# Modulation columns by one-column matmuls, later stores of three weight blocks, and weight subtractions on GpSimd

## The chip, the core and the metric

The kernel runs on one core of one Trainium2 chip. The metric is the device time of one execution in microseconds (us). A core has five engines that run side by side: TensorE (PE in the profile; its weight loads are a row of their own, PEld), VectorE (DVE), ScalarE (ACT), GpSimd (POOL) and SyncE (SP), which here issues nearly all DMAs. Each engine takes its own instructions strictly in the order in which they were written.

## The reference, cut to what matters

One encoder layer over 2048 tokens of width 1024. Six vectors of 1024 (shift, scale and gate for each of two sub-layers) come from a small product with the weight `w_ada`:

```python
c_act = jax.nn.silu(c)
mod = (c_act @ w_ada[l] + b_ada[l])[:, None, :]
sh1, sc1, g1, sh2, sc2, g2 = jnp.split(mod, 6, axis=-1)
h = x * (1.0 + sc1) + sh1
p = h @ w_in[l]                       # 1024 -> 3328 columns
# p is cut into a convolution module, four recurrence heads, chunked attention
y = jnp.concatenate([y_conv, y_rec, y_att], axis=-1) @ w_out[l]
x = layer_norm(ALPHA * x + (1.0 + g1) * y, ln1_g[l], ln1_b[l])
h = x * (1.0 + sc2) + sh2
gt, up = jnp.split(h @ w_ffn_in[l], 2, axis=-1)
y = (jax.nn.silu(gt) * up) @ w_ffn_out[l]
x = layer_norm(ALPHA * x + (1.0 + g2) * y, ln2_g[l], ln2_b[l])
```

All is fp32. Nothing can be projected before `sh1` and `sc1` are known.

## The kernel before, in words

The tokens are worked off in four quarters of 512 (`Q`). In each quarter the mixer does: the scaled input `h` as eight tiles `hh`/`hl` (`load_h`, line 233); 13 column blocks of 256 of the input projection (`proj_f` with 512-column matmuls at line 270, `proj_t` with 256-column matmuls at line 321); the convolution with 31 taps on each of two tiles (`conv_taps`, line 377, all on DVE); four recurrence heads (`rec_head`, lines 451 to 560); attention; and the output projection (`out_proj`). After that comes the FFN (lines 953 and 1095), which the change does not touch and which takes the second half of the time.

To keep fp32 precision each operand is split into a rounded high part (a cast on ACT, line 230) and the low rest (a subtraction, line 231), and three matmuls replace one. `load_w` (line 247) brings a weight block in four parts `kp` of 256 rows: it loads `wraw` (256 KB), casts, subtracts, and stores the pair as `wki` or `wko` (512 KB) to DRAM. In later quarters it loads the pair again and splits nothing. The part with even `kp` is subtracted on DVE, the odd one on GpSimd. There are four buffers `whl` for the pairs.

`start` (line 274) is the beginning of quarter one. For each `kp` it makes two columns of `sh1` and two of `sc1`: it loads four tiles `ada_w` of 256 rows, multiplies and adds them on DVE into `tmp` (lines 295 and 297, eight instructions for each of eight column pairs), and sums over the partitions by two matmuls with a column of ones (line 170). Then it scales two tiles of `x` and adds this `kp`'s share of the first three blocks (convolution gate, convolution value, first recurrence head; line 308).

The other modulation vectors are made by the generator `ada_rest` (line 708), one batch for each `next(rest)`: a batch loads eight tiles `xb` of `w_ada` and adds them up on DVE as `adac` (lines 159 and 161). The eight batches are spread over the heads of quarters one to three.

A scheduler puts the instructions of each engine in an order from priorities and its own estimate; the order is then fixed. An engine that waits in that order holds up all that stands behind.

Of the kernel before, what the change touches and what calls it, by code (L numbers as in the profile page):

```python
# [12 lines left out]
ALU = mybir.AluOpType  # L13
PSUM = bass.MemoryType.PSUM

P = 128
# [26 lines left out]
C_BSH1, C_BSC1, C_BSH2, C_BSC2 = 8, 16, 24, 32  # L43
# [65 lines left out]
def mixer_phase(tc, es, env):  # L109
    nc = tc.nc  # L110
    NQ = env["NQ"]
    x, xT, bias_d, w_ada, w_in, w_out, rows = (env[k] for k in ("x", "xT", "bias", "w_ada", "w_in", "w_out", "rows"))
    ident, ones, epsc, cact = (env[k] for k in ("ident", "ones", "epsc", "cact"))
    mod1, mod2, h2s, h2b, zst, zd, g1d, g2d = (
        env[k] for k in ("mod1", "mod2", "h2s", "h2b", "zst", "zd", "g1d", "g2d"))
    col = env["col"]
# [18 lines left out]
    def tmp(w=Q):  # L135
        return pt.tile([P, 640], F32, name="tmp", tag="tmp", bufs=N_TMP)[:, 0:w]
# [7 lines left out]
    def psum(name):  # L144
        return pm.tile([P, Q], F32, name=name, tag="pm")
# [22 lines left out]
    def cols_out(acc, ps, dst, one, bc, n=4):  # L168
        for j in range(n):
            nc.tensor.matmul(out=ps[:, j:j + 1], lhsT=acc[:, j * P:(j + 1) * P], rhs=ones[:, 0:1],  # L170
                             start=True, stop=True)
        nc.vector.scalar_tensor_tensor(out=dst, in0=ps[:, 0:n], scalar=one, in1=col(bc, n),
                                       op0=ALU.add, op1=ALU.add)
# [45 lines left out]
    for a in atm:  # L219
# [4 lines left out]
    wkept = {k: tc.dram_tile([4, P, 2, 2, 256], F32R, name=f"wk{k[0]}{k[1]}")  # L224
             for k in [("i", b) for b in range(D_IN // 256)] + [("o", b) for b in range(4)]}
    kept = set()
    state, uhist, kvprev = {}, {}, {}

    def split(src, hi, lo, eng=nc.vector):
        nc.scalar.copy(out=hi, in_=src)  # L230
        eng.tensor_tensor(out=lo, in0=src, in1=hi.bitcast(F32), op=ALU.subtract)  # L231
# [12 lines left out]
    def move(dst, src):  # L244
        nc.sync.dma_start(out=dst.bitcast(F32), in_=src.bitcast(F32))

    def load_w(key, order, eng=None):
        parts = {}
        src = (w_in if key[0] == "i" else w_out)[key[1]]
        for kp in order:  # L250
            w = pa.tile([P, 2, 2, 256], F32R, name="whl", tag="whl", bufs=N_W)
            parts[kp] = hi, lo = w[:, 0], w[:, 1]
            if (key, kp) in kept:
                move(w, wkept[key][kp])
                continue
            raw = pa.tile([P, 2, 256], F32, name="wraw", tag="wraw", bufs=N_WRAW)
            nc.sync.dma_start(out=raw, in_=src[:, kp * 2:kp * 2 + 2, :])
            split(raw, hi, lo, eng or (nc.gpsimd if kp % 2 else nc.vector))
            move(wkept[key][kp], w)
            kept.add((key, kp))  # L260
        return parts

    def proj_f(b):
# [10 lines left out]
    def start():  # L274
        nst = 0
        ps = {b: [pool.tile([P, Q], F32, name="pjt", tag=tag) for _ in range(2)]
              for b, pool, tag in ((B_AG, pj, "pj"), (B_AV, pj, "pj"), (B_REC, pm, "pm"))}
        for kp in range(4):
            c0 = kp * 256
            for part in range(2):  # L280
                acc = tmp(256)
                for kk in range(4):
                    i = nst % 22
                    nst += 1
                    if i >= 14:
                        st = pt.tile([P, 2, 256], F32, name="ada_w", tag=f"attk{i % 4}", bufs=2)
                    else:
                        st = pa.tile([P, 2, 256], F32, name="ada_w", tag=f"y{'hl'[i % 2]}{1 + i // 2}")
                    r0 = kk * 256
                    nc.sync.dma_start(out=st, in_=w_ada[r0:r0 + 256, part * D + c0:part * D + c0 + 256].rearrange(  # L290
                        "(k p) c -> p k c", p=P))
                    for k in range(2):
                        sc = cact[:, 2 * kk + k:2 * kk + k + 1]
                        if kk == 0 and k == 0:
                            nc.vector.tensor_scalar(out=acc, in0=st[:, k], scalar1=sc, scalar2=None, op0=ALU.mult)
                        else:
                            nc.vector.scalar_tensor_tensor(out=acc, in0=st[:, k], scalar=sc, in1=acc,
                                                           op0=ALU.mult, op1=ALU.add)
                o = part * 8 + kp * 2
                cols_out(acc, psum("mps"), mod1[:, o:o + 2], float(part),  # L300
                         (C_BSC1 if part else C_BSH1) + kp * 2, 2)
            load_h(0, (2 * kp, 2 * kp + 1))
            for n, b in enumerate(ps):
                w = load_w(("i", b), (kp,), nc.gpsimd if n else nc.vector)[kp]
                for k in range(2):
                    for j in range(2):
                        for n, (a, c) in enumerate(PASSES):
                            nc.tensor.matmul(out=ps[b][j], lhsT=w[a][:, k, j * P:(j + 1) * P],
                                             rhs=hts[2 * kp + k][c], start=(kp == 0 and k == 0 and n == 0),
                                             stop=(kp == 3 and k == 1 and n == 2))  # L310
        return ps
# [121 lines left out]
    def rec_v(hp):  # L433
        vp = proj_t(("i", B_RI + hp), hts, range(4))
        V = pr.tile([P, NB, 256], F32, name="recV", tag="recV", bufs=2)
        with shifted(tc, -BOOST):
            for i in range(2):
                nc.scalar.copy(out=V[:, 2 * i:2 * i + 2, :], in_=vp[i])
        return V
# [350 lines left out]
    rest = ada_rest()  # L790
    for q in range(NQ):
        us, k0, V, G = nxt
        if q == 2:
            h2_norm(tc, env, 0)
            h2_norm(tc, env, 1)
        taps = conv_taps(us)
        accs = None
        kbm = k0
        for h in range(4):
            rec_head(q, h, kbm, V, G[h % 2])  # L800
            for _ in range(TAPS[h] if h < 3 else 0):
                accs = next(taps, accs)
            if h == 2:
                conv_back(accs)
            if h < 3:
                kbm = rec_front(h + 1)
            if h == 1:
                V = rec_v(1)
                G = rec_g(1)
            if h < 3 or q == 0:  # L810
                next(rest, None)
            if q >= 2:
                for _ in range(2):
                    next(early, None)
        kvq = att_front(q)
        attention(q, kvq)
        if q + 1 == NQ:
            for _ in rest:
                pass
            as_.close()  # L820
            rs_.close()
            ffn_open(tc, env)
        else:
            nxt = fronts_a(q + 1)
        out_proj(q)
# [389 lines left out]
```

## Time and profile before

| | |
|---|---|
| median of three runs | 2602.72 us (2598.47 to 2602.81) |
| the profiled execution, its time | 2589.91 us |
| its span, first to last instruction | 2588.2 us |
| PE busy | 2457.8 us, 95% of the span |
| DVE busy | 1656.1 us, 64% |
| ACT / POOL busy | 997.2 us / 665.7 us |
| granted TensorE clock, mean | 0.974 |

The profile is one execution. The busy share of PE is a mean over stages: the FFN is almost full, and the holes lie in quarter one, at the end of quarter four and in the last microseconds. The granted clock has two levels, 1.2 and 2.4 GHz, which the views print as 0.5 and 1.0.

### The profile page before, as it was taken

How to read it: one execution, taken by the hardware profiler on the slowest of the kernel's cores; microseconds unless marked ns; L12 is line 12 of the kernel's file. 1: busy time of each engine (PE TensorE's matmuls, PEld its weight loads, DVE VectorE, ACT ScalarE, POOL GpSimd, SP SyncE). 2: the span in 40 equal slices, each digit the busy share in tenths (PEclk: the TensorE clock that was granted, in tenths of full speed). 3: DMA queues.
4: the chain of work that ended last, by engine and by line, in shares of the span. 5: the costliest groups of instructions: out<-in, count | busy, mean ns of one | idle time of the engine just before them, and what ended most of it. 6: DMA issues, size and time to landing. Idle time of an engine off the chain costs nothing.

```text
span 2588.2 us, 36360 instructions
## 1 busy us (share of the span) xinstructions
PE 2457.8 (95%) x13274; PEld 2078.5 (80%) x13274; DVE 1656.1 (64%) x2917; ACT 997.2 (39%) x1920; POOL 665.7 (26%) x571
## 2 busy tenths in 40 slices
PE   6888899999999999987999999999999999999998
PEld 5766799879977898876878788888888888888887
DVE  7987696669557785666655555765445474364666
ACT  2444444354244433544323333433333352242333
POOL 3433112200152112510333332332322211111121
PEclk8997999999999999988999999999999999999999
DMA  9676667663755645547333332442222274454544
GB/s 354 212 236 187 186 197 264 201 180 128 241 183 172 205 164 184 191 135 259 102 117 119 118 130 90 164 142 91 74 82 90 74 244 142 130 182 134 161 147 142
DMA packets 202691, 423.99 MB, mean 164 GB/s; under 512 B 20240, under 2 KB 69008, under 8 KB 202512
## 3 DMA queue, kind: packets, MB, share of 16 engines
q1 hardware_dynamic: 202352, 421.15, 49.8%
q8 instruction: 104, 1.70, 0.3%
q14 instruction: 75, 0.61, 0.1%
q0 software_dynamic: 160, 0.52, 0.1%
HBM read 317.78 MB, written 95.42 MB: 160 GB/s over the span
## 4 chain that ended last, share of the span: by engine, by line
PE 78%; DVE 10%; DMA 6%; issue 3%; ACT 2%; POOL 1%; SPq 0%; DVEq 0%; POOLq 0%; ACTq 0%
PE pi L953 31%; PE po L1095 17%; PE pjt L270 11%; PE pjt L321 9%; PE lp L513 2%; DVE cacc L377 2%; PE sc L625 1%; PE tp L661 1%; PE tp L648 1%; DMA whl<-wki 1%; DMA whl<-wko 1%; PE lp L533 1%; DMA xst<-zall 1%; DMA opraw<-srcd 1%; DMA xb<-in_x_dram 1%
## 5 line engine op out<-in xcount | busy, mean ns | idle before, releaser
L953 PE MATMUL pi<-oph,fhi 128*128 128x512 f32 x1232 | 484.1, 393 | 17.8 <-ACT fhi L829 11.9
L953 PE MATMUL pi<-opl,fhi 128*128 128x512 f32 x1232 | 483.7, 393 | 0.0
L953 PE MATMUL pi<-oph,flo 128*128 128x512 f32 x1232 | 478.9, 394 | 0.0
L270 PE MATMUL pjt<-hh,whl 128*128 128x512 f32 x1184 | 402.5, 411 | 16.2 <-DMA whl<-wki 6.4
L953 PEld LDWEIGHTS pi<-oph,fhi 128*128 128x128 f32 x1232 | 232.4, 189 | 70.2 <-ACT fhi L829 12.1
L829 ACT CAST fhi<-fraw 128x512 fp32r<-128x512 f32 x220 | 136.2, 621 | 392.3 <-PE pi L953 376.6
L270 PEld LDWEIGHTS pjt<-hh,whl 128*128 128x128 f32 x1184 | 227.4, 194 | 66.4 <-DMA whl<-wki 6.0
L958 DVE TENSOR_TENSOR fu<-fu,pi 128x512 f32<-128x512 f32 x176 | 120.8, 686 | 245.8 <-PE pi L953 245.1
L953 PEld LDWEIGHTS pi<-opl,fhi 128*128 128x128 f32 x1232 | 232.5, 189 | 52.3
L1095 PE MATMUL po<-oph,alo 128*128 128x512 f32 (+1 forms) x702 | 273.9, 390 | 0.0
L1095 PE MATMUL po<-oph,ahi 128*128 128x512 f32 (+1 forms) x702 | 270.1, 385 | 3.1 <-DVE res L1116 3.1
L1095 PE MATMUL po<-opl,ahi 128*128 128x512 f32 (+1 forms) x702 | 272.6, 388 | 0.0
L953 PEld LDWEIGHTS pi<-oph,flo 128*128 128x128 f32 x1232 | 232.3, 189 | 49.5 <-DVE flo L830 0.2
L830 DVE TENSOR_TENSOR alo<-araw,ahi 128x512 fp32r<-128x512 f32 x172 | 148.5, 871 | 190.9 <-ACT ahi L829 174.3
L270 PE MATMUL pjt<-hl,whl 128*128 128x512 f32 x592 | 243.0, 411 | 0.0
L321 PE MATMUL pjt<-whl,yh 128*128 128x256 f32 x1024 | 196.7, 288 | 15.5 <-DMA whl<-wko 12.0
L830 DVE TENSOR_TENSOR flo<-fraw,fhi 128x512 fp32r<-128x512 f32 x220 | 159.5, 742 | 70.9 <-ACT fhi L829 70.8
L377 DVE SCALAR_TENSOR_TENSOR cacc<-u,cs,cacc 128x512 f32<-128x512 f32 x240 | 195.3, 843 | 0.2
L829 ACT CAST ahi<-araw 128x512 fp32r<-128x512 f32 x172 | 104.9, 618 | 222.3 <-PE po L1095 208.0
L321 PEld LDWEIGHTS pjt<-whl,yh 128*128 128x128 f32 x1024 | 164.1, 194 | 17.7 <-DVE yl L231 7.9
L930 POOL TENSOR_TENSOR ft<-fraw 128x512 f32<-128x512 f32 x43 | 59.9, 1392 | 450.6 <-DMA fraw<-in_w_fi_dram 433.5
L1095 PEld LDWEIGHTS po<-oph,ahi 128*128 128x128 f32 x702 | 132.4, 189 | 31.7 <-DVE res L1116 3.3
(257 smaller groups left out, 4539.1 us busy)
## 6 DMA issues: line engine op xcount, KB each, us to landing
whl<-wki SPq DMA_DIRECT2D x156, 512.0 KB, 3.8
fraw<-in_w_fi_dram SPq DMA_DIRECT2D x86, 512.0 KB, 3.7
araw<-actd SPq DMA_DIRECT2D x154, 256.0 KB, 3.4
wki<-whl SPq DMA_DIRECT2D x52, 512.0 KB, 4.3
whl<-wko SPq DMA_DIRECT2D x48, 512.0 KB, 3.5
actd<-fs SPq DMA_DIRECT2D x44, 512.0 KB, 3.3
xb<-in_w_ada_dram SPq DMA_DIRECT2D x64, 256.0 KB, 4.7
opraw<-srcd SPq DMA_DIRECT2D x56, 256.0 KB, 5.0
```

Source lines behind the costliest of these rows:

```text
L270: nc.tensor.matmul(out=ps[j], lhsT=w[kt // 2][a][:, kt % 2, j * P:(j + 1) * P], rhs=hts[kt][c], start=(kt == 0 and n == 0), stop=(kt == KT ...
L321: nc.tensor.matmul(out=ps[tt // 2][:, tt % 2, :], lhsT=lhs[2 * kp + k][c][:, tt * P:(tt + 1) * P], rhs=w[kp][a][:, k, :], start=(ko == 0 a ...
L377: nc.vector.scalar_tensor_tensor(out=ac, in0=us[j][:, t:t + Q], scalar=col(wc + t), in1=ac, op0=ALU.mult, op1=ALU.add)
L513: nc.tensor.matmul(out=lp[0:n, c, :], lhsT=ddf[:, c * P:c * P + n], rhs=d4[:, c, :, :], start=True, stop=True)
L533: nc.tensor.matmul(out=lp[:, c, :], lhsT=K[:, 2 * i + c, :], rhs=M[:, 2 * i + c, :], start=True, stop=True)
L625: nc.tensor.matmul(out=sc[:, 0:n + x], lhsT=qs[hd][ph][:, i * P:(i + 1) * P], rhs=kt_[:, o - x0:o - x0 + n + x], start=ph == 0, stop=ph == 1)
L829: nc.scalar.copy(out=hi, in_=src)
L830: nc.vector.tensor_tensor(out=lo, in0=src, in1=hi.bitcast(F32), op=ALU.subtract)
L930: e.tensor_tensor(out=t1, in0=w12, in1=w11, op=ALU.subtract)
L953: nc.tensor.matmul(out=out, lhsT=w[n][a][:, idx, :], rhs=ops[n, idx][c], start=first and idx == 0 and i == 0, stop=idx == NK - 1 and i == ...
L958: nc.vector.tensor_tensor(out=out, in0=a, in1=b, op=ALU.add)
L1095: nc.tensor.matmul(out=pts[j][:, c], lhsT=a[x][:, j * P:(j + 1) * P], rhs=wo[f][y][:, c], start=f == 0 and m == 0, stop=f == NF - 1 and m ...
```

## The change

Three things are done. In `start` the DVE accumulation is gone: each `ada_w` tile is the stationary operand of four matmuls with one column of `cact` as the moving one, and the sum over all rows is made in PSUM; the final add reads it from there. `load_w` takes GpSimd for the subtraction wherever no engine is named, and the first three blocks are no longer stored in quarter one (`keep` is False there): in quarter two they are loaded raw again, split and stored. And the batches of `ada_rest` move: three fall into quarter one instead of four (one of them behind `att_front`), four into quarter two instead of three, and the last steps into quarter three.

```diff
-    def load_w(key, order, eng=None):
+    def load_w(key, order, eng=None, keep=True):
...
-            split(raw, hi, lo, eng or (nc.gpsimd if kp % 2 else nc.vector))
-            move(wkept[key][kp], w)
-            kept.add((key, kp))
+            split(raw, hi, lo, eng or nc.gpsimd)
+            if keep:
+                move(wkept[key][kp], w)
+                kept.add((key, kp))
...
-                acc = tmp(256)
+                mps = psum("mps")
                 for kk in range(4):
...
                     for k in range(2):
-                        sc = cact[:, 2 * kk + k:2 * kk + k + 1]
-                        if kk == 0 and k == 0:
-                            nc.vector.tensor_scalar(out=acc, in0=st[:, k], scalar1=sc, scalar2=None, op0=ALU.mult)
-                        else:
-                            nc.vector.scalar_tensor_tensor(out=acc, in0=st[:, k], scalar=sc, in1=acc,
-                                                           op0=ALU.mult, op1=ALU.add)
+                        for j in range(2):
+                            nc.tensor.matmul(out=mps[:, j:j + 1], lhsT=st[:, k, j * P:(j + 1) * P],
+                                             rhs=cact[:, 2 * kk + k:2 * kk + k + 1],
+                                             start=kk == 0 and k == 0 and j == 0, stop=kk == 3 and k == 1 and j == 1)
                 o = part * 8 + kp * 2
-                cols_out(acc, psum("mps"), mod1[:, o:o + 2], float(part),
-                         (C_BSC1 if part else C_BSH1) + kp * 2, 2)
+                nc.vector.scalar_tensor_tensor(out=mod1[:, o:o + 2], in0=mps[:, 0:2], scalar=float(part),
+                                               in1=col((C_BSC1 if part else C_BSH1) + kp * 2, 2),
+                                               op0=ALU.add, op1=ALU.add)
...
-                w = load_w(("i", b), (kp,), nc.gpsimd if n else nc.vector)[kp]
+                w = load_w(("i", b), (kp,), nc.gpsimd if n else nc.vector, False)[kp]
...
-            if h < 3 or q == 0:
+            if q == 1 or q == 2 and h % 2 or q == 0 and h > 1:
                 next(rest, None)
...
         kvq = att_front(q)
+        if q == 0:
+            next(rest, None)
         attention(q, kvq)
```

How the written order moves is shown at three places. The first is PE's order at the very beginning, before:

```order
L170 MATMUL mps<-ones,tmp 128x1 x4
L308 MATMUL pjt<-hh_312,whl 128x512 x6
L308 MATMUL pjt<-hl_313,whl 128x512
L308 MATMUL pjt<-hh_312,whl 128x512
L308 MATMUL pjt<-hl_313,whl 128x512
```

The same place in the change (the one-column matmuls are now line 295; `hh_322` and `hh_439` are the first tiles of the first and second `kp`; the stretches between are those of line 308):

```order
L295 MATMUL mps<-cact,ada_w 128x1 x32
L308 MATMUL pjt<-hh_322,whl 128x512 x6
L295 MATMUL mps<-cact,ada_w 128x1 x7
L308 MATMUL pjt<-hl_323,whl 128x512
...
L308 MATMUL pjt<-hh_329,whl 128x512
L295 MATMUL mps<-cact,ada_w 128x1 x39
L308 MATMUL pjt<-hh_439,whl 128x512 x6
L295 MATMUL mps<-cact,ada_w 128x1
```

Of the 128 one-column matmuls 32 now stand ahead of the first projection, and the other 96 in four longer runs of 7, 39, 32 and 17 (and a single one) between the 144 matmuls of line 308; in the order before, 16 such matmuls stood there.

The second place is DVE's order before, in the second recurrence head of quarter one, where two batches of `adac` stand among the head's steps (lines 462, 464, 466, 555 to 559 and 496 to 503):

```order
L464 COPY recel<-tmp 128x4
L466 TENSOR_TENSOR recqe<-tmp,recM 128x512
L161 SCALAR_TENSOR_TENSOR adac<-xb,cact,adac 128x512
L420 SCALAR_TENSOR_TENSOR ft<-pjt,ft 128x512
L421 SCALAR_TENSOR_TENSOR ft<-pjt,ft 128x512
L462 TENSOR_TENSOR tmp<-tmp,recK 128x512
L555 SCALAR_TENSOR_TENSOR tmp<-recG,tmp 128x512
L161 SCALAR_TENSOR_TENSOR adac<-xb,cact,adac 128x512
L556 SCALAR_TENSOR_TENSOR tmp<-tmp 128x512
L161 SCALAR_TENSOR_TENSOR adac<-xb,cact,adac 128x512
```

The same steps in the change:

```order
L464 COPY recel<-tmp 128x4
L466 TENSOR_TENSOR recqe<-tmp,recM 128x512
L462 TENSOR_TENSOR tmp<-tmp,recK 128x512
L555 SCALAR_TENSOR_TENSOR tmp<-recG,tmp 128x512
L556 SCALAR_TENSOR_TENSOR tmp<-tmp 128x512
L179 SCALAR_TENSOR_TENSOR xb<-rps,xb 128x512
L159 TENSOR_SCALAR adac<-xb,cact 128x512
L161 SCALAR_TENSOR_TENSOR adac<-xb,cact,adac 128x512
L558 TENSOR_TENSOR tmp<-tmp,recG 128x512
```

Between the ends of the first and second head (line 559) DVE had 53 instructions, 14 of them `adac`; now it has 39, three of them `adac`.

The third place is GpSimd's order from the first head on, before (line 493 is a head's work, line 231 a weight subtraction):

```order
L231 TENSOR_TENSOR whl<-wraw,whl 128x512 x4
L460 TENSOR_TENSOR tmp<-recB 128x512
L231 TENSOR_TENSOR whl<-wraw,whl 128x512 x2
L493 TENSOR_TENSOR tmp<-recB 128x512 x6
L526 TENSOR_TENSOR tmp<-recB 128x256
L231 TENSOR_TENSOR whl<-wraw,whl 128x512 x6
```

And in the change:

```order
L231 TENSOR_TENSOR whl<-wraw,whl 128x512 x6
L460 TENSOR_TENSOR tmp<-recB 128x512
L231 TENSOR_TENSOR whl<-wraw,whl 128x512 x4
L493 TENSOR_TENSOR tmp<-recB 128x512 x6
L526 TENSOR_TENSOR tmp<-recB 128x256
L231 TENSOR_TENSOR whl<-wraw,whl 128x512 x9
```

All subtractions now pass through this one queue, the head's steps between them. Over the whole program 28 subtractions leave DVE (32 before, 4 now), and GpSimd does 76 instead of 36, 12 of these for the three blocks that are split a second time.

## Rows read from the trace of the kernel before

**Rows 1.** The page, part 1: busy time, share and instructions by engine.

```profile
PE 2457.8 (95%) x13274; PEld 2078.5 (80%) x13274; DVE 1656.1 (64%) x2917; ACT 997.2 (39%) x1920; POOL 665.7 (26%) x571
```

**Rows 2.** Windows by stage: length, PE, PEld, DVE, ACT, POOL busy, PEclk, DMA share, GB/s.

```profile
16.40:68.10 51.70, 44.70 (x172) 35.22 (x173) 42.29 (x83) 14.67 (x26) 14.10 (x11) 0.87 1.01 363
68.10:165.70 97.60, 82.64 (x500) 70.59 (x499) 96.96 (x132) 47.40 (x96) 43.63 (x29) 0.95 0.61 196
165.70:207.70 42.00, 26.89 (x142) 21.88 (x143) 32.67 (x54) 19.51 (x42) 14.79 (x13) 0.81 0.85 293
...
241.90:299.70 57.80, 49.39 (x258) 40.81 (x257) 40.03 (x65) 31.42 (x63) 14.14 (x12) 0.89 0.68 190
...
400.00:565.80 165.80, 158.12 (x989) 135.81 (x989) 108.41 (x220) 79.57 (x169) 32.27 (x36) 0.99 0.65 209
```

**Rows 3.** Groups by line and shape, 0 to 70 us: the accumulation that goes.

```profile
L297 DVE SCALAR_TENSOR_TENSOR tmp<-ada_w,cact,tmp 128x256 f32<-128x256 f32 x56 | 28.7, 538 | 1.5 <-DMA ada_w<-in_w_ada_dram 0.7
```

**Rows 4.** Timeline of PE from 24 to 28 us.

```profile
24.29 0.39 PE L308 MATMUL pjt<-hh,whl 128*128 128x512 f32 x1
24.51 0.39 PE L308 MATMUL pjt<-hl,whl 128*128 128x512 f32 x1
...
26.78 0.95 PE L170 MATMUL mps<-ones,tmp 128*128 128x1 f32 x8
```

**Rows 5.** Timeline of PE from 11 to 20.5 us: start, length, instruction.

```profile
13.76 1.01 PE L170 MATMUL mps<-ones,tmp 128*128 128x1 f32 x4 [1.41 <-DVE tmp L297]
16.41 2.92 PE L308 MATMUL pjt<-hh,whl 128*128 128x512 f32 x6 [1.64 <-ACT hh L230]
...
19.57 0.63 PE L308 MATMUL pjt<-hh,whl 128*128 128x512 f32 x1
19.99 0.63 PE L308 MATMUL pjt<-hl,whl 128*128 128x512 f32 x1
```

**Rows 6.** Timeline of DVE from 4 to 9 us: the first `ada_w` tile.

```profile
4.27 0.35 DVE L295 TENSOR_SCALAR tmp<-ada_w,cact 128x256 f32<-128x256 f32 x1
```

**Rows 7.** Timeline of PE from 66.5 to 68.5 us: the last matmul of line 308.

```profile
67.67 0.40 PE L308 MATMUL pjt<-hh,whl 128*128 128x512 f32 x1
```

**Rows 8.** Windows from 205 to 229 us, columns as in Rows 2.

```profile
205.00:222.00 17.00, 14.32 (x70) 12.74 (x71) 15.81 (x36) 2.46 (x8) 0.00 (x0) 0.50 0.39 124
212.00:218.00 6.00, 6.00 (x25) 5.52 (x26) 5.63 (x14) 0.00 (x0) 0.00 (x0) 0.50 0.16 52
223.00:229.00 6.00, 6.00 (x30) 5.14 (x30) 3.14 (x7) 0.62 (x1) 1.17 (x1) 1.00 0.79 227
```

**Rows 9.** Groups of PE by line and shape, 208 to 218 us.

```profile
L513 PE MATMUL lp<-tmp 128*128 128x64 f32 x24 | 5.4, 422 | 1.1 <-DVE tmp L503 1.1
```

**Rows 10.** Groups of DVE and POOL by shape, 68.1 to 165.7 us.

```profile
L377 DVE SCALAR_TENSOR_TENSOR cacc<-u,cs,cacc 128x512 f32<-128x512 f32 x60 | 60.7, 1045 | 0.0
L231 DVE TENSOR_TENSOR whl<-wraw,whl 128x512 fp32r<-128x512 f32 x12 | 9.0, 752 | 0.6 <-ACT whl L230 0.6
...
L231 POOL TENSOR_TENSOR whl<-wraw,whl 128x512 fp32r<-128x512 f32 x13 | 21.2, 1632 | 48.1 <-ACT whl L230 38.1 <-PE ms L551 5.9 <-DMA wki<-whl 4.2
```

**Rows 11.** Lines 377 (60 to 200 us) and 230 by tile: ns minimum/median/maximum.

```profile
L377 DVE SCALAR_TENSOR_TENSOR cacc<-u,cs,cacc x60: 720/742/1786, 68.6 to 160.5; 128x512 f32<-128x512 f32 x60
...
L230 ACT CAST whl<-wraw x68: 598/619/643, 12.7 to 395.6; 128x512 fp32r<-128x512 f32 x68
```

**Rows 12.** Timelines of DVE and of POOL around 88 to 100 us.

```profile
88.36 7.69 DVE L377 SCALAR_TENSOR_TENSOR cacc<-u,cs,cacc 128x512 f32<-128x512 f32 x5
...
89.54 8.85 POOL L493 TENSOR_TENSOR tmp<-recB 128x512 f32<-128x512 f32 x6
```

**Rows 13.** Groups of DVE by shape, 165.7 to 207.7 us: the `adac` batches.

```profile
L161 DVE SCALAR_TENSOR_TENSOR adac<-xb,cact,adac 128x512 f32<-128x512 f32 x12 | 11.6, 967 | 6.3 <-DMA xb<-in_w_ada_dram 6.2
```

**Rows 14.** Timeline of PE from 185 to 210 us: two holes.

```profile
194.53 1.09 PE L469 MATMUL ktp<-ident,tmp 128*128 128x128 f32 x4 [6.26 <-DVE tmp L462]
...
205.64 1.09 PE L513 MATMUL lp<-tmp 128*64 128x64 f32 x8 [7.23 <-DVE tmp L501]
```

## The prediction

> **What bounds the kernel now.** I read the page's first part, then windows by stage, then the timelines of the stages that the change touches. PE is busy 95% of the span [rows 1], so what PE gets to do more is paid wherever no hole takes it, and a microsecond is won only where PE waits or runs at its lower clock. The stage view shows where that is [rows 2]. In the start (16.4 to 68.1 us) PE is busy 44.7 of 51.7 us at a clock of 0.87, the DMA engines are full (share 1.01) and DVE works 42.3 us. In the convolution stretch (68.1 to 165.7 us, to the end of the first recurrence head) DVE is the bound, busy 96.96 of 97.6 us. In the second head (165.7 to 207.7 us) PE works only 26.9 of 42 us at 0.81. In quarter two (400 to 565.8 us) PE is busy 158 of 165.8 us: work that falls there on another engine is hidden, and little can be won.
>
> **The start: PE gets the modulation sums.** Removed are 64 DVE instructions: 56 of 0.54 us [rows 3] and eight firsts, some 33 us of DVE. They stand beside DMA and PE and are not the last to be waited for once PE does the sums. Added are 128 one-column matmuls, removed 16. The price is in the trace, since line 170 has the same shape (128x128 fp32 weights, one column); one matmul there is two records. At the higher clock eight records take 0.95 us [rows 4], less the overlap of the last about 0.22 us a matmul; at the lower clock four take 1.01 us [rows 5], about 0.44. The matmuls of line 308 start every 0.43 us at the lower clock (19.57, 19.99) [rows 5] and every 0.22 to 0.23 (24.29, 24.51) at the higher [rows 4]. So a one-column matmul costs PE as much as a 512-column one: its time is the weight load.
>
> Now PE's new order, step by step.
>
> (a) 32 one-column matmuls stand ahead of everything. The first tile is there at 4.3 us [rows 6]. PE has not run, and line 170 at 13.76 shows the lower clock [rows 5]: 4.3 + 32 x 0.44 = 18.4 us. Before, the sums were done at 13.76 + 1.01 = 14.77, and 1.64 us later, after the scaling on DVE and a cast on ACT, the projection began at 16.41 [rows 5]. Now it begins at about 20: 3.6 us later.
>
> (b) Behind it PE has 144 matmuls of line 308 and 96 one-column ones. All at the higher clock: 144 x 0.227 + 96 x 0.22 = 32.7 + 21.1 = 53.8 us. To it come 2 us, since some ten matmuls run at 0.43 before the clock rises (as from 16.41 to the rows at 24 us), and 1.6 us, because the last 17 one-column matmuls stand directly ahead of the last 36 projections, which wait for the scaling. That ends at 20 + 53.8 + 3.6 = 77.4 us. Before, the last matmul of line 308 ended at 67.67 + 0.23 = 67.9 [rows 7]. Least loss: 9.5 us.
>
> (c) The clock. From 212 to 218 us PE is busy for all of 6.0 us and stays at 0.50 [rows 8]; what it does there is narrow matmuls, 24 of 64 columns with 128x128 weights among them [rows 9]. From 223 to 229 us, with 512-column matmuls, it is as busy, at 1.00. So PE that is busy with weight loads does not keep or raise its clock here. I take the first run of 7 one-column matmuls, half of the run of 39 and half of that of 32 at the lower level, 43 x 0.22 = 9.5 us, and eight projections behind each of the two long runs at 0.43, 16 x 0.2 = 3.2 us. End at about 90 us: 22 us later. If all 96 ran at the lower level and ten projections behind each of three runs, it would be 77.4 + 21.1 + 6 = 104.5, 36.6 us later. I choose 22, near the middle, since a run begins at the level that the projections left.
>
> The trace speaks here against a rule: the Trainium skill, "TensorE: Matmul & The Clock Gate", Part 1, ties the clock to how busy PE has been, and by that the one-column runs, which keep PE busy, would hold it at 2.4 GHz; the start would lose 9.5 us in place of 22.
>
> The 12 stores of the first three blocks (512 KB each) leave the full DMA queue in this stage. That would pay if DMA set its end; with PE at 90 us it doesn't, and I cost it at nothing. Nothing else can start earlier: the taps need the finished blocks.
>
> **The convolution stretch.** Twelve subtractions go from DVE (0.752 us each) to GpSimd, where one takes 1.63 us [rows 10]. DVE is the bound, so 12 x 0.75 = 9 us seem to be won. But the two disturb each other: a tap takes 0.742 us in the median [rows 11] and 1.045 in the mean over this stretch [rows 10], and while GpSimd makes six subtractions of its own in 8.85 us, five taps take 7.69 us, 1.54 each [rows 12]. Over the stretch the 60 taps lose 60.7 - 60 x 0.742 = 16.2 us to 43.6 us of GpSimd [rows 2, 10], or 0.37 a microsecond: 1.63 us cost DVE 0.6 us at that mean and 0.8 at the rate of those five taps. Twelve cost 7 to 10 us. Net -2 to +1; I take -2, with -9 (GpSimd costs nothing) and +10 (each costs all of its 1.63 us) as bounds.
>
> A sharper rule stands in the Trainium skill, "SBUF — State Buffer", section "Who interferes with whom": a DVE instruction with two SBUF inputs and a GpSimd instruction that reads SBUF exclude each other for the whole instruction. By it this stretch would end near the bound of +10.
>
> **The second and third head.** Of 14 `adac` instructions between the ends of the first two heads three stay, and fewer loads of `xb` (256 KB each) share the DMA engines. Twelve of line 161 took 11.6 us and made DVE wait 6.2 us for DMA [rows 13]. Behind them stood what PE waited for: 6.26 us for line 462 and 7.23 us for line 501 [rows 14], 13.5 us in all, and from 205 to 222 us PE then worked 14.3 us at 0.50 [rows 8], which is 7.2 us more than at full clock. So at most 20.7 us can come back. The head's own chain (GpSimd, ACT, DVE, PE in turn) stays; I take three quarters, -15, with 0 (another wait steps in) and -21 as bounds.
>
> **What is put elsewhere.** One batch comes behind the attention's projections (241.9 to 299.7 us), eight `adac` of 0.75 us. DVE works 40 of 57.8 us there [rows 2], so most hides; +2, at most +7 with its DMA waits. Quarter two takes one batch more, 12 casts of 0.62 us [rows 11], 12 subtractions, and 12 stores that SP issues among the loads. They hide under PE (158 of 165.8 us busy [rows 2], with ACT 79.6 and POOL 32.3); +1, at most +6 if a load is late behind a store. If PE's cover were gone, the subtractions alone would cost 12 x 1.5 = 18 us.
>
> **Sum.** +22 - 2 - 15 + 2 + 1 = +8 us. On the profiled execution's 2589.91 us that is 2598; it lies 12.8 us under the median of the runs shown, to which I add the same 8: 2611 us.
>
> **Rivals.**
> - *The clock stays up in the start* (the other side). If the one-column runs don't lower it, the start costs 9.5 us and the sum is -4.5: 2598 us. For it speaks that the projections between the runs are dense; against it the busy 6 us at 0.50 [rows 8]. It decides as soon as the start loses under 14 us, for then the sum is no longer positive. Chance 0.15. The rule of the Trainium skill, "TensorE: Matmul & The Clock Gate", Part 1, would give this case.
> - *The holes of the second head close wholly and the stretch gains its 9 us*: 22 - 9 - 21 + 1 = -7, 2596 us. For it speaks that both of PE's waits stood behind `adac`; against it the five taps beside GpSimd [rows 12]. Chance 0.12.
> - *GpSimd excludes DVE for all of its time*: +10 in place of -2, so +20: 2623 us. For it speaks the tap of 1.54 us, against it the mean over the stretch. Chance 0.14. The rule of the Trainium skill, "SBUF — State Buffer", "Who interferes with whom", would give this case.
> - *A new wait takes the hole's place*: on GpSimd 22 subtractions, where 13 stood, now come between the end of the start and the second head's line 493, so that line 493 stands behind subtractions that wait for a cast, and PE waits as before: +23, 2626 us. Chance 0.14.
>
> **How the numbers follow.** My forecast has 0.45. No change means within 0.2% (5.2 us), about what a measurement of this kernel can tell. The forecast's own range is 2600 to 2622: of its 0.45 I put 0.28 over the bound, 0.12 within, 0.05 below. The first rival lies at the lower bound (0.08 faster, 0.07 same), the second is faster (0.11 and 0.01), the last two slower (0.28). Together faster 0.24, same 0.2, slower 0.56. The range for 8 in 10 goes from the second rival and a little below, 2594, to the last one with a start on its dear side, 2632.
>
> **What would show it.** Right: the last matmul of line 308 ends near 90 us; the clock is at 0.5 in part of the runs of line 295; DVE is still full in the convolution stretch with taps as slow as now; the waits for lines 462 and 501 in the second head shrink by more than half; quarter two is as long as before. Wrong: an end of the start before 80 us or a clock that stays at 1.0 there; or a convolution stretch that is clearly shorter than 97.6 us, which would mean that GpSimd costs DVE less than I read.

## The result and the profile after

The kernel became slower: 2630.02 us in the median (2625.72 to 2635.03, four runs) against 2602.76 us of the kernel before (four runs), a ratio of 1.0106 with a 95% interval of 1.0079 to 1.0133. The same kernel, run again among the experiments on another chip, gave 1.0168 (1.0147 to 1.0189). I had forecast 2611 us and slower; the range up to 2632 holds the median.

The profiled execution has a span of 2631.3 us, 43.1 more than before. The medians are only 27 apart: the profiled execution of the kernel before took 2589.91 us, 13 less than its median. Its page, part 1, which answers to [rows 1]:

```profile
PE 2502.8 (95%) x13498; PEld 2122.6 (81%) x13498; DVE 1626.9 (62%) x2825; ACT 1002.0 (38%) x1932; POOL 721.7 (27%) x611
```

PE is busy 45 us longer, at 224 records more: 256 of line 295 come, 32 of line 170 go. The windows by stage, in the columns of [rows 2]: the start, the convolution stretch, the second, third and fourth head of quarter one, and quarter two:

```profile
19.60:95.40 75.80, 74.25 (x336) 65.19 (x336) 15.11 (x27) 12.65 (x23) 15.31 (x12) 0.80 0.51 167
95.40:196.10 100.70, 81.01 (x462) 71.44 (x462) 94.16 (x116) 44.58 (x87) 59.87 (x38) 0.85 0.53 173
196.10:236.50 40.40, 37.06 (x192) 30.50 (x191) 22.43 (x41) 18.99 (x40) 17.88 (x15) 0.92 0.62 191
236.50:275.00 38.50, 33.35 (x223) 29.18 (x222) 25.80 (x43) 18.10 (x40) 15.86 (x16) 0.91 0.71 238
275.00:336.20 61.20, 47.71 (x225) 37.17 (x224) 47.13 (x77) 34.18 (x68) 23.15 (x20) 0.86 0.69 210
432.00:595.40 163.40, 153.77 (x952) 132.93 (x953) 114.83 (x227) 74.98 (x162) 37.72 (x38) 0.96 0.64 211
```

The start was 51.7 us long with full DMA engines; now it is 75.8 us, PE is busy in 74.25 of them at a clock of 0.80, the DMA share is down to 0.51 and DVE works 15 us. So PE sets the end of the start, and it is late by 27.4 us. In the second head PE now works 37.06 of 40.4 us where it worked 26.9 of 42 [rows 2]; yet the stage is only 1.6 us shorter.

What became of the 27 us is seen best from marks that I read from the timelines of every kernel (lines are counted as in the kernel before). The table has the difference to the first profile of the kernel before, in us: the end of the last matmul of line 308; the start of line 559, the last step of a head, in the first, second and fourth head of quarter one; the end of line 704, the last step on DVE in the output projection, of quarters one and two; line 559 of the third head of quarter three; the end of the span. The second line is the kernel before itself, in another execution, up to 4 us off; the two executions of the change differ by up to 6. So much is scatter.

| kernel | start | head 1 | head 2 | head 4 | out 1 | out 2 | head 3 of q3 | end |
|---|---|---|---|---|---|---|---|---|
| before (absolute) | 68.1 | 165.7 | 207.7 | 299.7 | 408.7 | 689.3 | 802.4 | 2588.2 |
| before_again | 0 | 0 | 0 | 0 | -3 | -2 | -2 | -4 |
| the change | +27 | +30 | +29 | +36 | +32 | +39 | +46 | +43 |
| after_again | +24 | +26 | +23 | +31 | +26 | +34 | +42 | +43 |
| only_cols | +27 | +28 | +31 | +30 | +30 | +32 | +33 | +30 |
| no_cols | 0 | +2 | -4 | +3 | +3 | +9 | +17 | +11 |
| wide | +5 | +4 | +3 | +11 | +6 | +14 | +19 | +17 |
| only_gps | -1 | -8 | -2 | +6 | +10 | +13 | +9 | +12 |
| gps_early | +1 | -6 | +2 | +7 | +7 | +8 | +8 | +7 |
| gps_late | 0 | +1 | -2 | -7 | -3 | +1 | -1 | -4 |
| only_rest | 0 | -1 | -5 | -10 | -21 | -18 | -4 | -5 |
| only_keep | 0 | -2 | +2 | +5 | -2 | -1 | 0 | -1 |
| keep_rest | 0 | 0 | +5 | +1 | -5 | +5 | +11 | +11 |
| early_keep_rest | -1 | +2 | +2 | +2 | -2 | +2 | +8 | +11 |

### The profile page after: what moved, and what is told of

The parts are those of the page before. It is cut to its first block, busy times and chain, and to the rows that moved or that the text cites. A ratio compares the mean times of both kernels' runs of the same rounds, so it can differ in the third digit from the quotient of the medians.

```text
span 2631.3 us, 36805 instructions
## 1 busy us (share of the span) xinstructions
PE 2502.8 (95%) x13498; PEld 2122.6 (81%) x13498; DVE 1626.9 (62%) x2825; ACT 1002.0 (38%) x1932; POOL 721.7 (27%) x611
## 4 chain that ended last, share of the span: by engine, by line
PE 80%; DVE 10%; DMA 6%; issue 2%; ACT 2%; POOL 0%; SPq 0%; DVEq 0%; ACTq 0%; POOLq 0%
PE pi L955 31%; PE po L1097 17%; PE pjt L271 11%; PE pjt L321 9%; DVE cacc L377 3%; PE lp L513 2%; PE mps L295 2%; PE pjt L308 2%; PE sc L625 1%; PE tp L661 1%; PE tp L648 1%; DMA whl<-wki 1%; DMA opraw<-srcd 1%; DMA ft<-in_xT_dram 1%; PE lp L533 1%
## 5 line engine op out<-in xcount | busy, mean ns | idle before, releaser
L377 DVE SCALAR_TENSOR_TENSOR cacc<-u,cs,cacc 128x512 f32<-128x512 f32 x240 | 202.4, 875 | 0.2
L231 POOL TENSOR_TENSOR whl<-wraw,whl 128x512 fp32r<-128x512 f32 x76 | 113.2, 1493 | 206.8 <-ACT whl L230 189.8
```

Source lines behind the costliest of these rows:

```text
L377: nc.vector.scalar_tensor_tensor(out=ac, in0=us[j][:, t:t + Q], scalar=col(wc + t), in1=ac, op0=ALU.mult, op1=ALU.add)
```

## The start, read step by step

PE's timeline from 0 to 97 us, the runs of one-column matmuls and the two places where PE waited (start, length, instruction; two records are one matmul; the stretches between are those of line 308):

```profile
4.34 13.78 PE L295 MATMUL mps<-cact,ada_w 128*128 128x1 f32 x64 [4.34 <-DVE cact L154]
19.61 2.92 PE L308 MATMUL pjt<-hh,whl 128*128 128x512 f32 x6 [1.48 <-ACT hh L230]
22.33 2.98 PE L295 MATMUL mps<-cact,ada_w 128*128 128x1 f32 x14
34.72 14.04 PE L295 MATMUL mps<-cact,ada_w 128*128 128x1 f32 x78
51.32 0.42 PE L295 MATMUL mps<-cact,ada_w 128*128 128x1 f32 x2
59.94 9.15 PE L295 MATMUL mps<-cact,ada_w 128*128 128x1 f32 x64
80.10 3.85 PE L295 MATMUL mps<-cact,ada_w 128*128 128x1 f32 x34
85.49 2.93 PE L308 MATMUL pjt<-hh,whl 128*128 128x512 f32 x6 [1.54 <-ACT hh L230]
```

Windows of the run of 39 one-column matmuls, the projections behind it, the run of 32, the projections behind it, the run of 17 and the last projections (columns as in [rows 2]):

```profile
34.80:48.70 13.90, 13.90 (x80) 13.90 (x78) 9.02 (x14) 1.75 (x3) 1.59 (x1) 0.60 0.91 304
48.80:59.80 11.00, 11.00 (x38) 8.89 (x39) 0.00 (x0) 1.24 (x2) 2.48 (x2) 0.74 0.21 75
60.00:69.00 9.00, 9.00 (x66) 9.00 (x64) 2.71 (x6) 1.76 (x3) 1.26 (x1) 0.77 0.30 89
69.10:80.00 10.90, 10.90 (x36) 8.72 (x37) 0.00 (x0) 1.24 (x2) 2.58 (x2) 0.72 0.08 26
80.20:83.90 3.70, 3.70 (x35) 3.66 (x33) 0.16 (x1) 0.62 (x1) 1.27 (x1) 1.00 0.43 154
85.50:95.40 9.90, 9.90 (x36) 7.78 (x36) 0.66 (x1) 3.03 (x7) 2.18 (x2) 0.84 0.03 11
```

Within a long run the clock falls. Two windows of the run of 32:

```profile
62.00:64.00 2.00, 2.00 (x21) 2.00 (x20) 0.16 (x1) 0.00 (x0) 0.00 (x0) 1.00 0.48 140
...
66.00:68.00 2.00, 2.00 (x11) 2.00 (x11) 0.00 (x0) 0.00 (x0) 1.08 (x1) 0.50 0.37 120
```

The first 32 one-column matmuls take 13.78 us, 0.43 each, and the projection begins at 19.61, 3.2 us later than before. The other 96 take 2.98 + 14.04 + 0.42 + 9.15 + 3.85 = 30.4 us. The last 17 of them cost 3.85 / 17 = 0.226 each, the price at the higher clock (1.00 in their window); at that price all 96 would take 21.7. In the run of 39 PE is busy without a gap, and the mean clock over it is 0.60, so it spent most of the run at the lower level. The 144 projections behind take the rest, 75.8 - 30.4 - 1.5 (the wait at 85.49) = 43.9 us, 0.305 each in place of 0.227: each stretch has its part at the lower level (0.74 and 0.72 behind the two long runs, 0.84 behind the wait).

## The experiments

The experiments ran on three chips, beside 23 or 35 runs of the kernel before on each. There its median was 2587 to 2589 us, 14 to 15 less than in the first result, so only ratios are compared.

**only_cols and no_cols: the one-column matmuls alone, and all but them.** The edit of only_cols is the part of the diff that lies in `start`'s loop over `part`; no_cols undoes just that.

> The kernel before with the modulation columns by one-column matmuls and nothing else. Theory 1 (PE pays in the start, since 240 one-column records go on its full queue and half of them run at 1.2 GHz): the last matmul of line 307 ends 25 to 30 us later than 67.9 us, and the time is 18 to 30 us above before (2620 to 2633). Rival (the loss sits in the moved batches and in GpSimd's queue, and the late start is taken up by the DVE-bound stretch behind it): 0 to 10 us above before.

> The change without the one-column matmuls: DVE adds up the modulation again, the rest of the change stays. Theory 1: the start ends no later than 68 us, and the time is 0 to 15 us below before (2588 to 2603), since 12 stores leave a full DMA queue. Rival: 10 to 25 us above before (2613 to 2628).

only_cols: 2619.43 us, 1.0119 (1.0087 to 1.015). no_cols: 2600.11 us, 1.0049 (1.0032 to 1.0065). With the one-column matmuls the start ends 27 us late, without them on time, and the loss stays nearly constant to the end (+27, +28, ... +33, +30): nothing behind the start takes it up. This part alone costs 1.2%. The other parts together, which I had expected to win up to 15 us, are no gain but cost 0.5%, which my sum did not have.

**wide: does the clock or the number of matmuls make the loss?** The same number of matmuls with the same weights, but the moving operand is the column of `cact` read 128 times; the add reads every 128th column of PSUM.

```diff
-                            nc.tensor.matmul(out=mps[:, j:j + 1], lhsT=st[:, k, j * P:(j + 1) * P],
-                                             rhs=cact[:, 2 * kk + k:2 * kk + k + 1],
+                            nc.tensor.matmul(out=mps[:, j * 128:(j + 1) * 128], lhsT=st[:, k, j * P:(j + 1) * P],
+                                             rhs=cact[:, 2 * kk + k:2 * kk + k + 1].broadcast_to([P, 128]),
...
```

> The change with a 128-column moving operand (the same column of cact 128 times) in place of one column; of the 128 equal sums one is read. If a record costs its 128x128 fp32 weight load (0.112 us at 2.4 GHz with one column, and 0.11 for the 128-column line 474) and the low clock is what narrow matmuls bring, then each record costs the same, the clock stays at 2.4 GHz behind the first rise, the start ends near 80 us in place of 95, and the time is 12 to 16 us below the change (about 2615). Rival (the clock falls for another reason, or a wide moving operand is paid): start at 95 us or later, time of the change (2630) or above.

2610.77 us, 1.0084 (1.0057 to 1.0111) against 1.0106 and 1.0168 of the change. The start ends at 73.0 us instead of 95.5. PE's timeline of wide, its longest runs:

```profile
4.25 9.36 PE L295 MATMUL mps<-cact,ada_w 128*128 128x128 f32 x64 [4.25 <-DMA ada_w<-in_w_ada_dram]
...
26.75 9.32 PE L295 MATMUL mps<-cact,ada_w 128*128 128x128 f32 x82
...
44.37 7.97 PE L295 MATMUL mps<-cact,ada_w 128*128 128x128 f32 x70
```

And its windows over the last two and the projections between:

```profile
26.80:36.00 9.20, 9.20 (x84) 9.20 (x83) 2.13 (x6) 2.37 (x4) 3.80 (x3) 1.00 1.09 356
36.10:44.30 8.20, 8.20 (x38) 6.76 (x37) 3.35 (x5) 1.86 (x3) 1.99 (x2) 1.00 1.02 328
44.40:52.30 7.90, 7.90 (x72) 7.90 (x71) 5.32 (x10) 1.76 (x3) 1.71 (x2) 1.00 0.85 302
```

With 128 times the columns a matmul costs 9.32 / 41 = 0.227 us, no more than in the last one-column run, and the clock stays at 1.00 throughout. PE is as busy in both kernels, and its order is nearly the same (behind the first 32, runs of 8, 41, 35 and 10 in place of 7, 39, 32 and 17). So 22.5 of the 27.4 us come from the clock (18.8 if taken from after_again's 91.8), and the matmuls as such cost 5. The rule by which PE's busy time holds the clock (the Trainium skill, "TensorE: Matmul & The Clock Gate", Part 1) does not fit these two traces if busy is read as the busy column: 13.9 of 13.9 us at 0.60 in the one, 9.2 of 9.2 at 1.00 in the other.

**only_rest: the moved batches alone.** The edit is the last two changed places of the diff.

> The kernel before with the batches of the other modulation vectors moved as in the change, nothing else. If PE's two waits of 6.3 and 7.2 us in the second head come back as time, as my step of -15 us said: 8 to 15 us below before (2588 to 2595). Rival (PE is owed the same projections and only does them at another place; the hole closes but nothing is won): within 5 us of before.

2587.23 us, 0.9997 (0.9979 to 1.0014): no change, where I had expected 8 to 15 us. Yet the second head did what I had forecast. Its windows, from the end of the first head to that of the second and on to that of the third:

```profile
165.20:203.00 37.80, 37.51 (x205) 31.79 (x203) 25.61 (x40) 18.45 (x36) 16.38 (x14) 1.00 0.82 265
203.00:239.60 36.60, 32.58 (x204) 27.80 (x204) 25.79 (x51) 17.75 (x36) 6.44 (x6) 0.95 0.80 265
```

PE is busy in 37.51 of 37.8 us at 1.00; of the two holes of [rows 14] one is gone, and of the other 3.3 us are left (at 206.27 us, behind that window). The kernel is 10 us ahead at the fourth head and 21 at the first output projection, more than the 15 of my sum. That is won and not only owed, for PE has done as many records up to there. It is lost again by the end of quarter three's output projection. Windows from 0 to these two ends, of the kernel before (first two lines) and of only_rest:

```profile
0.00:408.70 408.70, 346.93 (x2038) 296.94 (x2039) 336.40 (x614) 168.53 (x361) 122.31 (x121) 0.92 0.72 236
0.00:980.60 980.60, 899.73 (x5833) 784.79 (x5834) 743.90 (x1491) 412.45 (x889) 230.75 (x241) 0.95 0.64 208
0.00:388.20 388.20, 338.35 (x2033) 289.88 (x2034) 327.25 (x609) 168.70 (x363) 121.54 (x121) 0.95 0.73 243
0.00:975.60 975.60, 894.55 (x5831) 778.94 (x5832) 740.60 (x1491) 410.70 (x889) 228.81 (x241) 0.97 0.63 209
```

Up to the first end PE idled for 61.8 us before and for 49.9 in only_rest; up to the second for 80.9 and 81.1. So the 12 us of idle time that the moved batches save are gone by then. PE's timeline of only_rest shows what stands there now:

```profile
749.63 1.13 PE L178 MATMUL rps<-adac,ones 128*128 128x512 f32 x2 [3.76 <-DVE adac L161]
```

and in the change, at 805.34 us, PE waits for the same batch, and in the next stretch for line 179, the add behind it (engine, line, waited for: us in all, times, longest; 727.8 to 848.9 us, and 848.9 to 1028 us):

```profile
PE rps L178 <- DVE adac L161: 3.6, 1, 3.6
```

```profile
PE pjt L271 <- DVE xb L179: 3.8, 1, 3.8
```

Line 178 closes four of the eight batches and line 170 the other four; these matmuls stand in PE's order among the projections. Where the batch's DVE sum is late, PE stops, and so a batch carries its hole to the place to which it is moved. In only_rest such waits are 9 of the 12 us: 3.8 at line 178 and 3.8 for line 179 in quarter three, and 1.5 at line 170 in quarter two. The kernel before has none of them behind its first output projection.

The third head of quarter three is no fair mark for this. Between the second output projection and that head the kernel before takes 113.1 us, the change 121.1, and the other kernels with the moved batches 5 to 13 us more than before; but all of them have done 47 records of PE more by then, those of the start apart. In the change PE's busy time makes up the whole difference (116.1 us with 711 records, 107.9 with 634).

**only_gps, gps_early, gps_late: the subtractions on GpSimd.** only_gps has `eng or nc.gpsimd` in `load_w` and nothing else. gps_early does it for the first six blocks behind the start (12 subtractions), gps_late for the later ones (16):

```diff
-            split(raw, hi, lo, eng or (nc.gpsimd if kp % 2 else nc.vector))
+            split(raw, hi, lo, eng or (nc.gpsimd if kp % 2 or len(kept) < 36 else nc.vector))
```

> The kernel before with all of quarter one's unnamed weight subtractions on GpSimd, nothing else. The change without its one-column matmuls was 0.49% above before, and the moved batches alone 0.03% below it. If the exchange of 0.75 us on DVE for 1.6 us on GpSimd with its disturbance is even, as my step of -2 us says: within 0.15% of before. Rival (GpSimd's one queue holds up heads and weight parts): 0.3 to 0.6% above.

> The kernel before, with GpSimd's subtractions for the first six blocks behind the start alone (the convolution stretch and the start of the second head): 12 leave DVE, the other 16 stay there. All 28 together ended the first head 8.2 us earlier and gave 1.0045 in the end. Theory (the loss is made behind the stretch, where head steps and output projection wait for subtractions in GpSimd's queue): the first head ends about 8 us earlier and most of it stays to the end, ratio 0.996 to 0.999. Rival (the gain of the stretch is only owed projection work, which PE pays in the second and third head): the 8 us are gone by the end of the third head, ratio 0.999 to 1.002. Second rival (the 12 of the stretch make the loss too): 1.003 to 1.005.

> The complement: the kernel before with GpSimd's subtractions only from the seventh block behind the start on (16 leave DVE). The first head ends as before (165.7 us). Theory (loss made behind the stretch): +10 to +15 us between the second head and the output projection of quarter one, ratio 1.004 to 1.007. Rivals (loss comes with the first 12): within 0.2% of before.

only_gps: 2599.88 us, 1.0045 (1.0029 to 1.0061). gps_early: 2595.15 us, 1.0018 (1.0002 to 1.0034). gps_late: 2583.47 us, 0.9979 (0.9963 to 0.9994), the lowest ratio of all. The theory that the loss is made behind the stretch by subtractions in GpSimd's queue has fallen: those of gps_late cost nothing. But 1.0018 and 0.9979 do not make up 1.0045, so that the 12 of the stretch make the loss is not shown either. In only_gps the stretch itself is 7 us shorter, 90.6 us. Windows of that stretch, and the groups of the taps and of GpSimd's subtractions in it, which answer to [rows 10]:

```profile
67.30:157.90 90.60, 75.03 (x445) 65.76 (x444) 90.22 (x112) 42.49 (x83) 51.08 (x34) 0.89 0.60 198
```

```profile
L377 DVE SCALAR_TENSOR_TENSOR cacc<-u,cs,cacc 128x512 f32<-128x512 f32 x60 | 61.8, 1076 | 0.0
...
L231 POOL TENSOR_TENSOR whl<-wraw,whl 128x512 fp32r<-128x512 f32 x21 | 33.0, 1579 | 36.5 <-ACT whl L230 35.5 <-POOL whl L231 0.9
```

The 60 taps take 61.8 us for 60.7 before, 1.1 more, while GpSimd makes 21 subtractions where it made 13 and DVE is relieved of 9 us. But PE does less in it (445 records, 500 before), at a lower clock, and pays that in the next heads. So it is in gps_early, which is 6 us early at the first head: its second head takes 49.1 us for 42.0, since PE does 180 records there for 142 and idles hardly less (13.9 us for 15.1). The third head then has 6.8 us of idle time for 1.1. PE's waits in both:

```profile
204.97 2.08 PE L178 MATMUL rps<-adac,ones 128*128 128x512 f32 x2 [7.04 <-DVE adac L161]
...
211.71 1.08 PE L513 MATMUL lp<-tmp 128*64 128x64 f32 x8 [2.96 <-DVE tmp L501]
...
227.47 1.86 PE L170 MATMUL mps<-ones,adac 128*128 128x1 f32 x8 [4.42 <-DVE adac L161]
```

The first stands at the end of the second head, the others in the third. The batches of `adac`, here still in their old places, are what PE waits for: 7.0 and 4.4 us. only_gps has the wait at line 178 too, 5.8 us at 204.07, and by its first output projection PE has idled 9.8 us longer than before.

**only_keep, keep_rest, early_keep_rest: the other parts, and the best of them together.** only_keep is the `keep` argument alone; keep_rest adds the moved batches; early_keep_rest adds gps_early's edit for the same six blocks.

> The kernel before with the first three blocks stored in quarter two, nothing else. If the stores, casts and subtractions hide under PE in quarter two, as my step of +1 us says: within 0.15% of before, start no longer. Rival (they hold up loads and weight parts where PE is full): 0.3 to 0.6% above, lost between the first and second output projection.

> The kernel before with the two parts of the change that did not lose: the stores of the first three blocks in quarter two, and the moved batches. If the two add up, 0.9984 x 0.9997 = 0.998; if the hole that the moved batches close is given back in the same place, 0.998 to 1.000. The start ends at 68 us.

> The same two parts, and GpSimd's subtractions for the first six blocks behind the start. By the theory that the loss is made behind the stretch the three add up: 0.994 to 0.997, the fastest of all kernels here. By the rival that PE pays the stretch's gain back in the heads: as the run without it, 0.998. By the second rival: 1.001 to 1.003.

only_keep: 2583.92 us, 0.9984 (0.9971 to 0.9998). keep_rest: 2599.99 us, 1.0033 (1.0019 to 1.0048), where I had expected 0.998 to 1.000. early_keep_rest: 2596.31 us, 1.0029 (1.0012 to 1.0045), where the theory gave 0.994 to 0.997 and the second rival 1.001 to 1.003. The start ends at 68.3 us in only_keep: 12 stores fewer in a full DMA queue do not bring its end forward. Two parts that alone give 0.9984 and 0.9997 give 1.0033 together, half a per cent from their product. And early_keep_rest is no worse than keep_rest, with a first head that is 2 us late where gps_early's was 6 us early. So parts of a few tenths of a per cent don't add up here. Each moves the order, and I take it that this moves the holes; that is not shown.

**before_again and after_again: the scatter.** Both kernels unchanged.

> The kernel before, for a second profile on this chip: how far stages of one kernel differ from execution to execution. Both theories: start ends at 68 us again; if the loss of the change behind the first quarter (8 to 15 us in the profiles) is scatter, this profile differs from the first by as much in the same stages.

> The change once more, on the chip and beside the same runs of before as the parts below, so that they can be set against each other. Both theories: about 1.0106 times before, as measured first.

before_again stays within 0.4 us of the first profile up to the second head and within 4 us at the end. after_again gave 1.0168 (1.0147 to 1.0189), with its start at 91.8 us where the first profile had 95.5. The parts of the change measured alone sum to 1.19 + 0.45 - 0.16 - 0.03 = 1.45%, between the 1.06 and the 1.68 that the change measured.

## Why the prediction was right, and where its steps were not

- **The start, +22: right in mechanism, 27.4 measured.** Of its parts: beginning 3.6 us later, measured 3.2; the one-column runs 21.1 + 9.5 = 30.6 us, measured 30.4; the wait ahead of the last projections 1.6, measured 1.5. The mis-sized term is the projections behind the runs: I gave them 32.7 + 2 + 3.2 = 37.9 us, they took 43.9. I had let eight projections behind each of two runs pay for the lower level, but every stretch paid: 36 projections and a one-column matmul took 11.0 us, the next 36 took 10.9 and the last 36 took 9.9, where 0.227 each makes 8.2 to 8.4. That the sum for the runs fits so well is in part luck: by their lengths an estimated 26 of the run of 39 were at the lower level and 9 of that of 32, and I had said half of each. The rival in which the clock stays up has fallen by the 0.60 in the run of 39, and wide shows that it is the clock: with it kept up the start costs 5 us.
- **The stores at nothing in the start: right** (only_keep, 68.3 us for 68.1).
- **The convolution stretch, -2: measured +3 in the change** (100.7 us for 97.6). Alone, GpSimd's part makes the stretch 7 us shorter, near the bound of -9; but it costs 10 us by the first output projection. In the change DVE is busy 94 of 100.7 us and no longer full, against what I had named as a sign of being right. Inside, the taps suffer as forecast where the two engines meet. DVE's and POOL's timelines of the change, 125 to 146 us:

```profile
124.81 16.26 DVE L377 SCALAR_TENSOR_TENSOR cacc<-u,cs,cacc 128x512 f32<-128x512 f32 x12
141.00 1.48 DVE L496 TENSOR_TENSOR tmp<-tmp,recK 128x256 f32<-128x256 f32 x1
142.40 0.41 DVE L501 TENSOR_TENSOR tmp<-tmp,recM 128x256 f32<-128x256 f32 x1
142.73 0.74 DVE L377 SCALAR_TENSOR_TENSOR cacc<-u,cs,cacc 128x512 f32<-128x512 f32 x1
```

```profile
125.58 1.79 POOL L231 TENSOR_TENSOR whl<-wraw,whl 128x512 fp32r<-128x512 f32 x1 [1.90 <-ACT whl L230]
127.34 8.83 POOL L493 TENSOR_TENSOR tmp<-recB 128x512 f32<-128x512 f32 x6
136.13 1.06 POOL L526 TENSOR_TENSOR tmp<-recB 128x256 f32<-128x256 f32 x1
137.16 5.04 POOL L231 TENSOR_TENSOR whl<-wraw,whl 128x512 fp32r<-128x512 f32 x3
```

  Twelve taps take 16.26 us beside a GpSimd that is busy from 125.58 on, 1.36 each, and 0.74 as soon as it stops: 7.4 us are lost. Line 501 stands behind them in DVE's order, and PE waits for it; only_gps, where nothing but the subtractions changed, has such a wait too (second view, PE's waits from 67.3 to 157.9 us: us in all, times, longest):

```profile
142.96 1.09 PE L513 MATMUL lp<-tmp 128*64 128x64 f32 x8 [12.21 <-DVE tmp L501]
```

```profile
PE lp L513 <- DVE tmp L501: 9.4, 1, 9.4
```

  Before, the longest such wait in this stretch was 4.4 us (PE's waits, 68.1 to 165.7 us):

```profile
PE lp L513 <- DVE tmp L501: 6.8, 2, 4.4
```

  So the cost of sharing reaches PE less through the length of the stretch than through a step of the head that queues behind slowed taps. Against the rival that GpSimd excludes DVE for all of its time speaks only_gps: with eight subtractions more there the taps take 1.1 us more, not 8 x 1.58 = 12.6. But where the two meet, each delays the other: from 125.58 to 142.20 us both are busy throughout, 16.6 us. By the median of a tap, 0.74, and the shortest times of line 493 and of a subtraction in the trace before, 1.04 and 1.27, the same work makes an estimated 20 us one behind the other and 12 side by side.
- **The second and third head, -15: the step that failed.** The holes closed as forecast: PE's wait for line 501 at the old place is 1.4 us (at 198.04), and it waits for line 462 no more. Alone this was worth 21 us at the first output projection. But in the change the two heads together are 3 us longer up to the end of the third (from 76.2 to 78.9 us). PE did 38 records fewer in the stretch (462 for 500), where the 12.2 us hole had opened, and then 50 more in the second head (192 for 142) and 48 more in the third, whose window before is:

```profile
207.70:241.90 34.20, 33.06 (x175) 28.55 (x176) 21.63 (x45) 10.30 (x20) 2.85 (x4) 0.79 0.57 172
```

  From the end of the start to the first output projection PE idles 4.8 us longer in the change than before, where only_rest alone saves 11.8. I counted a closed hole as time won and did not ask what PE still owed; and my sum had no term for the places in quarters two and three to which the batches move, where only_rest loses again what it had saved. The rival in which the holes close wholly and the stretch wins 9 us has its two halves only in separate runs. The last rival, a new wait on GpSimd, has the number (+23, and +28 with a start of 27) but not the mechanism: PE idles 3.3 us in the second head, and the new wait stands in the stretch, behind slowed taps.
- **The batch behind the attention's projections, +2:** 3.4 us measured (61.2 for 57.8), within its bounds. **Quarter two, +1:** 163.4 us for 165.8 up to its last head, but PE is busy in fewer of them, and its output projection ends 6 us later against before than the first one's, which is my bound of +6. only_keep, which moves only the stores, casts and subtractions there, loses 1 us; the kernels with the moved batches lose 3 to 10.
- **The sum.** +8 us was forecast; the ratio makes +28 in the first result (0.0106 x 2602.7) and +44 in the second, because a start of +27 was not paid back by the heads. The sign rested on the start, which every run with one-column matmuls confirms. That the range holds the result is in part luck: its upper end of 2632 came from the last rival, and with the second result's ratio the time would be 2646 us.

What stays open: why keep_rest loses where its parts don't, why only_gps loses more than gps_early and gps_late together, and so how much of the remaining 0.5% is any one edit's. The order of all engines changes with each edit; that this alone makes 0.3% is a guess. gps_late, at 0.9979, has the lowest ratio; after so many variants of one per mille or two I would not call that more than a hint.

## What to carry to other kernels

Here matmuls with one moving column cost PE as much as wide ones, and long runs of them lowered the clock of the projections behind them too (0.74 and 0.72). Where a narrow matmul must be, try it with more columns, and price both the run and what follows. A hole that closes is a gain only if the engine owes nothing from elsewhere, and work that is moved can take its hole along: follow it to its new place and cost that. Two kernels are compared at a mark up to which the engine has done the same work, so count its records there. When the parts of a change are each worth some tenths of a per cent, measure them in combination, for their sum says little.

## What was not expected of the hardware

A 128-column fp32 matmul costs as much as a one-column one (0.227 and 0.226 us at the higher clock), so the wide form was free here, and the clock stayed at 1.00 with it. And the column of the granted clock does not show the slow beginning. The window of the change's first one-column run:

```profile
4.30:18.20 13.90, 13.78 (x64) 13.73 (x64) 1.31 (x6) 1.85 (x3) 7.26 (x16) 1.00 1.03 337
```

It prints 1.00, while the matmuls take 0.43 us each, the pace of the lower level. In wide the same first 32 take 9.36 us: the higher pace came during the run, with 6 records a microsecond at first and 11 from 9.3 us on. For the first microseconds the spacing of the matmuls is the better witness.
